# Decay logits as one 128-row matmul and gate columns made later in a one-core encoder layer

## The chip, the core and the metric

The kernel runs on one core of a Trainium2 chip. The metric is the device time of one execution in microseconds (us), lower is better. The core has a tensor engine (PE, with its weight loads listed as PEld), a vector engine (DVE), a scalar engine (ACT), GpSimd (POOL) and a sync engine (SP) that here only issues DMAs. Each engine works through its own queue in order; semaphores tie the queues together.

## The reference, cut to what matters

Two sequences of 256 tokens (stacked here to 512 columns) pass through one layer of width 1024: a feed-forward block, a mixer, a second feed-forward block and a norm. The mixer adds a gated linear attention (GLA, four heads) and an mLSTM (four heads), each scanned forwards and backwards. The change is in the gates of the two:

```python
# GLA: decay logits per direction from a 16-wide projection lr, then log-sigmoid
lr_f, lr_b = jnp.split(lr, [GLA_LOWRANK], axis=-1)
la_f = jax.nn.log_sigmoid((lr_f @ w2_f + b2_f).astype(f32)) / GLA_TAU
la_b = jax.nn.log_sigmoid((lr_b @ w2_b + b2_b).astype(f32)) / GLA_TAU
# mLSTM: two input gates and two forget gates per head
ig_f, lf_f = gates[:, :, 0], jax.nn.log_sigmoid(gates[:, :, 1])
ig_b, lf_b = gates[:, :, 2], jax.nn.log_sigmoid(gates[:, :, 3])
```

## The kernel before, in words

All tokens lie along the free dimension: a tile is 128 features by 512 tokens. To keep float32 accuracy with the faster `fp32r` matmul, each operand is split into a rounded high part (ACT copies it to `fp32r`) and the rest as low part (DVE subtracts), and a product is the sum of three matmuls: high by high, high by low, low by high (`mm3`, lines 202 to 204, with weights split in `split_w`, lines 93 and 94).

The order of work within each engine is not written by hand. A planner takes the program in text order and gives each engine, as it becomes free in the planner's own model of time, the earliest instruction in the text that is ready; the resulting queues are fixed in the program. An instruction is also held until a buffer of its kind is free. Tiles named `z`, `cc_ps`, `gA`, `gB`, `ops_g` and `mS` share four score buffers in PSUM (`scp`), given out in the order of the text.

The stretch around the change, in text order:
- The first feed-forward block ends; for each of its eight output tiles ACT makes the split input of the mixer and the squares, and POOL adds up the squares (`add_sq`, line 199).
- The mixer's pools open (lines 409 to 419): `w2s` (the second factor of the decay projection, one tile per direction), masks, and two zeroed tiles `zz`. Their DMAs are issued from POOL. Then the row norm (`rms_stat`: matmuls `st_m` line 160 and `sp_m` line 173) and the gemm `small`, whose result `ss` has in rows 0 to 31 the 16-wide projections of both directions, in rows 32 to 63 the same again, and from row 64 the mLSTM gates.
- Lines 430 to 438: rows 0 to 31 of `lr` are the high part of the projection, rows 32 to 63 the low part. `w2h` (64 rows) holds the high part of the factor twice, `w2l` (32 rows) its low part.
- `gla_half(0)` (heads 0 and 1): for each head the gemms of query and key, then `gla_prep`, where for each direction two matmuls (lines 519 and 520, 64 and 32 rows) make the decay logits `z`; ACT and DVE turn them into running sums and scaled queries and keys. Then the values gemm (`values`, `gemm_t`: lines 460 to 462, with `whi_vg` and `wlo_vg`), then `gla_weights` (`gA`, `gB`) and `gla_values` (`ops_g`).
- Gate rows of the mLSTM (lines 606 to 660), a long chain of small DVE operations on 8 rows, ending in `gR` (ACT, line 659) and `gN`. Lines 661 to 666: four matmuls turn `gR` into columns `cc_ps`, which DVE copies to `cc`. Line 669: `gN` goes to DRAM, from where the mLSTM part reads it broadcast.
- `gla_half(1)` (heads 2 and 3), line 671, then the mLSTM part, whose weights (`mlstm_weights`, line 717) read `cc` and the broadcast `gN`.

Of the kernel before, what the change touches and what calls it, by code (L numbers as in the profile page):

```python
# [9 lines left out]
F32 = mybir.dt.float32  # L10
F32R = mybir.dt.float32r
I32 = mybir.dt.int32
AF = mybir.ActivationFunctionType
ALU = mybir.AluOpType
# [4 lines left out]
T = 512  # L19
# [17 lines left out]
def encoder_kernel(ctx: ExitStack, tc: tile.TileContext, xT, par, w2, gnorm, mask,  # L37
                   w_f1, w_o1, w_small, w_mix, w_tm, w_out, w_f2, w_o2, out):
    nc = tc.nc
# [6 lines left out]
    dp = ctx.enter_context(tc.tile_pool(name="dp", bufs=1, space=bass.MemoryType.DRAM))  # L46
# [4 lines left out]
    @contextmanager  # L51
    def pools(**sizes):
        with ExitStack() as es:
            for n, b in sizes.items():
                stage[n] = es.enter_context(tc.tile_pool(name=f"{n}_{len(opened)}", bufs=b, reuse_waits="tile"))
                opened.append(n)
            yield
            for n in sizes:
                del stage[n]
# [3 lines left out]
    def slab(name, dt=F32, shape=(P, T)):  # L63
        return sp.tile(list(shape), dt, tag="slab", name=name)

    def mslab(name, dt=F32, shape=(P, T)):
        return stage["ms"].tile(list(shape), dt, tag="mslab", name=name)
# [4 lines left out]
    def mtmp(name, shape=(P, T)):  # L72
        return stage["mt"].tile(list(shape), F32, tag="mtmp", name=name)
# [7 lines left out]
    def scp(name, shape=(P, T)):  # L81
        return pc.tile(list(shape), F32, tag="sc", name=name)
# [55 lines left out]
    def col(c):  # L138
        return pt[:, c:c + 1]
# [75 lines left out]
    def gemm(src, xs, name, wide=False):  # L215

        ps = acc(f"ps_{name}", wide)
        for k, (hi, lo) in enumerate(chunks(src, len(xs), name)):
            mm3(ps, hi, lo, xs[k][0], xs[k][1], k == 0, k == len(xs) - 1)
        return ps  # L220
# [187 lines left out]

    mixer_stage = ExitStack()
    mixer_stage.enter_context(pools(wp=3, ms=16, mt=6))  # L410
    w2s = [mslab(f"w2s{d}", F32, (64, T)) for d in range(2)]
    masks = mslab("masks", I32, (P, 4, P))
    cm, am = masks[:, 0:2, :], masks.bitcast(F32)[:, 2:4, :]
    zz = [mslab(f"zz{i}", F32, (P, 4, P)) for i in range(2)]
    for z in zz:
        nc.gpsimd.memset(z, 0.0)
    for d in range(2):
        nc.gpsimd.dma_start(w2s[d], w2[:, d * T:(d + 1) * T])
    nc.gpsimd.dma_start(masks, mask)
    rm, rc_m = rms_stat(sqm, "m")  # L420
    rcol = cp.tile([P, 4], F32, name="rcol")
# [5 lines left out]
    ss = slab("ss")  # L427
    nc.vector.tensor_tensor(out=ss, in0=ps, in1=rm, op=ALU.mult)

    lr, lrh = slab("lr", F32R, (64, T)), slab("lrh", F32R, (64, T))  # L430
    nc.scalar.copy(lr[0:32, :], ss[0:32, :])
    nc.scalar.copy(lrh[32:64, :], ss[32:64, :])
    nc.vector.tensor_tensor(out=lr[32:64, :], in0=ss[32:64, :], in1=lrh.bitcast(F32)[32:64, :], op=ALU.subtract)
    w2h = [slab(f"w2h{d}", F32R, (64, T)) for d in range(2)]
    w2l = [slab(f"w2l{d}", F32R, (32, T)) for d in range(2)]
    for d in range(2):
        nc.scalar.copy(w2h[d], w2s[d])
        nc.vector.tensor_tensor(out=w2l[d], in0=w2s[d][0:32, :], in1=w2h[d].bitcast(F32)[0:32, :], op=ALU.subtract)

    def neg_softplus(dst_m, dst_l, src, bias):  # L440

        with tc.issue_after(log_exp):
            nc.scalar.activation(dst_l, src, AF.Abs, bias=bias)
            nc.scalar.activation(dst_l, dst_l, AF.Exp, scale=-1.0)
            nc.scalar.activation(dst_l, dst_l, AF.Ln, bias=1.0)
        nc.vector.tensor_scalar(out=dst_m, in0=src, scalar1=bias, scalar2=0.0, op0=ALU.add, op1=ALU.min)
# [67 lines left out]
    def gla_prep(h, qh, kh):  # L514
        E = []
        for d in range(2):
            zp = scp(f"z{d}{h}")
            f = slice(h * P, (h + 1) * P)
            nc.tensor.matmul(zp, lhsT=w2h[d][:, f], rhs=lr[0:64, :], start=True, stop=False)
            nc.tensor.matmul(zp, lhsT=w2l[d][:, f], rhs=lr[0:32, :], start=False, stop=True)  # L520
            m_, l_ = mtmp(f"zm{d}{h}"), mtmp(f"zl{d}{h}")
            neg_softplus(m_, l_, zp, col(C_B2 + 4 * d + h))
            b = mtmp(f"zb{d}{h}")
            for c in range(4):
                s = slice(c * P, (c + 1) * P)
                o_, i0, i1 = b[:, s], m_[:, s], l_[:, s]
                if d:
                    o_, i0, i1 = o_[:, ::-1], i0[:, ::-1], i1[:, ::-1]
                nc.vector.tensor_tensor_scan(out=o_, data0=i0, data1=i1, initial=0.0,
                                             op0=ALU.add, op1=ALU.subtract)  # L530
            b4 = b.rearrange("p (c t) -> p c t", t=P)

            qc, kc = (1, 0) if d == 0 else (0, 1)
            edge = (P - 1) if d == 0 else 0
            ex = mslab(f"ex{d}{h}", F32, (P, 2, 2, P))
            eq = mslab(f"eq{d}{h}", F32, (P, 4, P))
            ek = mslab(f"ek{d}{h}", F32, (P, 4, P))
            q4 = qh.rearrange("p (c t) -> p c t", t=P)
            k4 = kh.rearrange("p (c t) -> p c t", t=P)
            nc.scalar.activation(ex[:, 0], b4[:, qc::2, :], AF.Exp, scale=TAU_INV)  # L540
            nc.vector.tensor_tensor(out=ex[:, 1], in0=b4[:, kc::2, :],
                                    in1=b4[:, kc::2, edge:edge + 1].broadcast_to([P, 2, P]), op=ALU.subtract)
            nc.scalar.activation(ex[:, 1], ex[:, 1], AF.Exp, scale=-TAU_INV)
            nc.vector.tensor_tensor(out=ek, in0=b4, in1=b4[:, :, 63 + d:64 + d].broadcast_to([P, 4, P]),
                                    op=ALU.subtract)
            nc.scalar.activation(eq, ek, AF.Exp, scale=TAU_INV)
            nc.scalar.activation(ek, ek, AF.Exp, scale=-TAU_INV)
            nc.vector.tensor_tensor(out=eq, in0=eq, in1=q4, op=ALU.mult)
            nc.vector.tensor_tensor(out=ek, in0=ek, in1=k4, op=ALU.mult)
            nc.vector.tensor_tensor(out=ex[:, 0], in0=ex[:, 0], in1=q4[:, qc::2, :], op=ALU.mult)  # L550
            nc.vector.tensor_tensor(out=ex[:, 1], in0=ex[:, 1], in1=k4[:, kc::2, :], op=ALU.mult)
            E.append((eq, ek, ex))
        return E
# [24 lines left out]
    def gla_values(h, v):  # L578
        for q in range(2):
            hi, lo = pp_g[h][q]  # L580
            ops = scp(f"ops_g{q}{h}", (P, 2, SEQ))
            for c in range(2):
                pv(ops[:, c, :], [((hi[:, 2 * s + c, :], lo[:, 2 * s + c, :]), [p[:, h % 2, :] for p in v[2 * q + s]])
                                  for s in range(2)])
            for c in range(2):
                nc.scalar.copy(o_slot(0, h, 2 * q + c), ops[:, c, :])
                head_sq(0, h, 2 * q + c, ops[:, c, :])

    def gla_half(n):
        E = {}  # L590
        for h in (2 * n, 2 * n + 1):
            qh, kh = slab(f"gq{h}"), slab(f"gk{h}")
            nc.vector.scalar_tensor_tensor(out=qh, in0=gemm(w_mix[h], xsm, f"gq{h}"), scalar=DK_SCALE, in1=rm,
                                           op0=ALU.mult, op1=ALU.mult)
            nc.vector.tensor_tensor(out=kh, in0=gemm(w_mix[4 + h], xsm, f"gk{h}"), in1=rm, op=ALU.mult)
            E[h] = gla_prep(h, qh, kh)
        v = values(n, f"vg{n}", False)
        pp_g.extend(gla_weights(h, E[h]) for h in (2 * n, 2 * n + 1))
        for h in (2 * n, 2 * n + 1):
            gla_values(h, v)  # L600
# [5 lines left out]
    def grow(name, w=T):  # L606
        return slab(name, shape=(8, w)) if w == T else cp.tile([8, w], F32, name=name)

    gI, gM, gL, gF, gF2, gN = (grow(n) for n in ("gI", "gM", "gL", "gF", "gF2", "gN"))
# [28 lines left out]
    for q in range(2):  # L638
        for (c, tot) in ((2 * q, gT), (2 * q + 1, gT2)):
# [6 lines left out]
                                op=ALU.add)  # L646
# [5 lines left out]
                                in1=gT2[:, 2 * q + 1:2 * q + 2], op=ALU.add)  # L652
# [5 lines left out]
    nc.vector.tensor_scalar(out=gN2, in0=gN2, scalar1=-88.0, scalar2=None, op0=ALU.max)  # L658
    nc.scalar.activation(gE, gN2, AF.Exp, scale=-1.0)
    nc.vector.tensor_scalar(out=gN, in0=gN, scalar1=-1.0, scalar2=None, op0=ALU.mult)  # L660
    cc_ps = scp("cc_ps", (P, 4, 24))
    for t in range(4):
        nc.tensor.matmul(cc_ps[:, t, :], lhsT=gR[:, t * P:(t + 1) * P], rhs=pt[:, C_ROW:C_ROW + 24],
                         start=True, stop=True)
    cc = cp.tile([P, 3, 4, 8], F32, name="cc")
    nc.vector.tensor_copy(cc.rearrange("p i t r -> p t i r"), cc_ps.rearrange("p t (i r) -> p t i r", i=3))

    d_nm = dp.tile([8, T], F32, name="d_nm")
    nc.gpsimd.dma_start(d_nm, gN)

    gla_half(1)
    head_r = [head_rms(0), None]


# [148 lines left out]
    for kp in range(4):  # L823
        t = (w_raw, w_sum)[kp % 2](f"second{kp}").rearrange("p a b -> p (a b)")
        t = t.rearrange("p (i m f) -> p i m f", i=2, m=NF)
# [131 lines left out]
```

## Time and profile before

| | us |
|---|---|
| Median of 3 runs | 1236.21 (1231.79 to 1238.27) |
| The profiled execution | 1234.58 |
| Span of its trace | 1232.8 |
| PE busy in the span | 1190.1 |
| DVE busy | 765.1 |
| ACT busy | 609.3 |
| POOL busy | 100.5 |
| Mean granted clock of PE | 0.983 of 2.4 GHz |

Times in the profile count from the start of the span. A row of the timeline gives the start, the duration, the engine, the line of the kernel, the operation, the tile written and the tiles read, and behind that the time its engine sat idle before it and what ended that. Matmuls are pipelined, so the distance from one start to the next says more than the duration shown. The granted clock is 1.00 for 2.4 GHz and 0.50 for 1.2 GHz.

### The profile page before, as it was taken

The numbers are of one execution on the slowest core, as the hardware profiler recorded it, in microseconds if no ns is written. First come the engines' busy times: TensorE is split into PE (matmuls) and PEld (weight loads), VectorE is DVE, ScalarE is ACT, GpSimd is POOL, SyncE is SP. The second block draws the span as 40 slices with busy tenths as digits, with TensorE's granted clock in tenths as the row PEclk, the third lists the DMA queues.
The fourth block names the chain that finished last, engine by engine and source line by source line (L and its number), as shares of the span: only waits on it lengthen the run. The fifth ranks groups of instructions, "written<-read, shape, count | busy, mean of one in ns | idle before, by whom it ended". The sixth has DMA issues, their size and how long they took to land.

```text
span 1232.8 us, 17190 instructions
## 1 busy us (share of the span) xinstructions
PE 1190.1 (97%) x6803; PEld 1035.0 (84%) x6803; DVE 765.1 (62%) x1159; ACT 609.3 (49%) x995; POOL 100.5 (8%) x114
## 2 busy tenths in 40 slices
PE   8899999999999999999999999999989999999996
PEld 6788899889987786888888888887879899989985
DVE  7976467557646788647565354464886457656643
ACT  5664256336536545566663232353565146426541
POOL 4000000000021002111000000012000000000011
PEclk9889999999999998999999999998999999999998
DMA  7355256436513212232323333224355246535512
GB/s 234 78 135 147 95 129 163 126 114 154 139 67 120 81 48 64 91 121 65 98 73 98 101 96 111 86 69 116 88 139 154 89 116 165 145 99 147 153 45 69
DMA packets 56737, 136.52 MB, mean 111 GB/s; under 512 B 5160, under 2 KB 19496, under 8 KB 56656
## 3 DMA queue, kind: packets, MB, share of 16 engines
q1 hardware_dynamic: 48480, 110.38, 28.1%
q0 software_dynamic: 6368, 22.68, 10.7%
q10 hardware_dynamic: 1808, 2.36, 0.6%
q8 instruction: 53, 0.87, 0.3%
q14 instruction: 28, 0.23, 0.1%
HBM read 133.29 MB, written 2.11 MB: 110 GB/s over the span
## 4 chain that ended last, share of the span: by engine, by line
PE 85%; DVE 6%; issue 3%; ACT 3%; DMA 2%; POOL 0%; POOLq 0%; DVEq 0%; SPq 0%; ACTq 0%
PE psy_f L302 17%; PE psq_f L302 8%; PE psz_f L302 4%; PE ps_f1o L202 3%; PE ps_f1o L203 3%; PE ps_f1o L204 3%; PE ps_f2o L203 3%; PE ps_f2o L202 3%; PE ps_f2o L204 3%; PE pt_ga L461 2%; PE pt_ga L460 2%; PE pt_ga L462 2%; PE pt_gb L461 2%; PE pt_gb L460 2%; PE pt_gb L462 2%
## 5 line engine op out<-in xcount | busy, mean ns | idle before, releaser
L302 PE MATMUL psy_f<-xch_f,wah_f1s 128*128 128x256 f32 x228 | 65.5, 287 | 3.8 <-DVE f1t L321 1.4
L302 PE MATMUL psy_f<-xch_f,wal_f2s 128*128 128x256 f32 x228 | 64.9, 285 | 4.2 <-DMA wal_f2s<-in_w_f 4.2
L302 PE MATMUL psy_f<-xch_f,wah_f2s 128*128 128x256 f32 x228 | 64.8, 284 | 0.1
L302 PE MATMUL psy_f<-xch_f,wal_f1s 128*128 128x256 f32 x228 | 64.6, 284 | 0.0
L302 PE MATMUL psy_f<-xcl_f,wah_f2s 128*128 128x256 f32 x228 | 64.5, 283 | 0.0
L302 PE MATMUL psy_f<-xcl_f,wah_f1s 128*128 128x256 f32 x228 | 64.5, 283 | 0.0
L460 PE MATMUL pt_ga<-whi_ga,xh_m 128*128 128x512 f32 x128 | 50.7, 396 | 0.0
L461 PE MATMUL pt_ga<-wlo_ga,xh_m 128*128 128x512 f32 x128 | 50.7, 396 | 0.0
L461 PE MATMUL pt_gb<-wlo_gb,xh_m 128*128 128x512 f32 x128 | 50.7, 396 | 0.0
L460 PE MATMUL pt_gb<-whi_gb,xh_m 128*128 128x512 f32 x128 | 50.5, 395 | 0.0
L462 PE MATMUL pt_ga<-whi_ga,xl_m 128*128 128x512 f32 x128 | 50.4, 394 | 0.0
L462 PE MATMUL pt_gb<-whi_gb,xl_m 128*128 128x512 f32 x128 | 50.2, 394 | 0.0
L94 DVE TENSOR_TENSOR wlo_ga<-raw_ga,whi_ga 128x1024 fp32r<-128x1024 f32 x16 | 19.6, 1225 | 46.2 <-ACT whi_ga L93 46.2
L302 PEld LDWEIGHTS psy_f<-xch_f,wah_f1s 128*128 128x128 f32 x228 | 43.8, 192 | 5.0 <-DVE f1t L321 1.7
L302 PEld LDWEIGHTS psy_f<-xch_f,wal_f2s 128*128 128x128 f32 x228 | 43.5, 191 | 4.6 <-DMA wal_f2s<-in_w_f 4.6
L385 DVE SCALAR_TENSOR_TENSOR x<-ps_f2o,x 128x512 f32<-128x512 f32 x23 | 15.9, 690 | 49.6 <-PE ps_f2o L204 49.6
L302 PEld LDWEIGHTS psy_f<-xcl_f,wah_f1s 128*128 128x128 f32 x228 | 44.0, 193 | 0.1
L385 DVE SCALAR_TENSOR_TENSOR x<-ps_f1o,x 128x512 f32<-128x512 f32 x24 | 16.6, 690 | 44.3 <-PE ps_f1o L204 44.3
L302 PEld LDWEIGHTS psy_f<-xch_f,wah_f2s 128*128 128x128 f32 x228 | 43.4, 190 | 0.6 <-ACT f2m L351 0.5
L302 PEld LDWEIGHTS psy_f<-xch_f,wal_f1s 128*128 128x128 f32 x228 | 43.7, 192 | 0.0
L302 PEld LDWEIGHTS psy_f<-xcl_f,wah_f2s 128*128 128x128 f32 x228 | 43.4, 190 | 0.1
L94 DVE TENSOR_TENSOR wlo_gb<-raw_gb,whi_gb 128x1024 fp32r<-128x1024 f32 x16 | 19.6, 1224 | 36.1 <-ACT whi_gb L93 36.0
(1083 smaller groups left out, 4052.4 us busy)
## 6 DMA issues: line engine op xcount, KB each, us to landing
raw_f1s<-in_w_f SPq DMA_DIRECT2D x19, 512.0 KB, 3.6
wal_f1s<-in_w_f POOLq DMA_DIRECT2D x19, 512.0 KB, 5.7
raw_f2s<-in_w_f SPq DMA_DIRECT2D x19, 512.0 KB, 3.6
wal_f2s<-in_w_f POOLq DMA_DIRECT2D x19, 512.0 KB, 5.5
raw_ga<-in_w_tm SPq DMA_DIRECT2D x16, 512.0 KB, 3.6
raw_gb<-in_w_tm SPq DMA_DIRECT2D x16, 512.0 KB, 3.5
sum_f1s<-in_w_f SPq DMA_DIRECT2D x19, 256.0 KB, 3.3
raw_f1s<-in_w_f SPq DMA_DIRECT2D x19, 256.0 KB, 4.0
```

What stands on the lines that cost most here:

```text
L94: nc.vector.tensor_tensor(out=lo[:, :width], in0=raw[:, :width], in1=hi.bitcast(F32)[:, :width], op=ALU.subtract)
L202: nc.tensor.matmul(ps, lhsT=wh, rhs=xh, start=start, stop=False)
L203: nc.tensor.matmul(ps, lhsT=wh, rhs=xl, start=False, stop=False)
L204: nc.tensor.matmul(ps, lhsT=wl, rhs=xh, start=False, stop=stop)
L302: nc.tensor.matmul(ps, lhsT=l[:, f], rhs=m, start=start and k == n == 0, stop=stop and k == 3 and n == 2, skip_group_check=True)
L385: nc.vector.scalar_tensor_tensor(out=x[i], in0=ps, scalar=0.5, in1=x[i], op0=ALU.mult, op1=ALU.add)
L460: nc.tensor.matmul(pss[t], lhsT=xh, rhs=hi[:, ws], start=k == 0, stop=False)
L461: nc.tensor.matmul(pss[t], lhsT=xh, rhs=lo[:, ws], start=False, stop=False)
L462: nc.tensor.matmul(pss[t], lhsT=xl, rhs=hi[:, ws], start=False, stop=k == KD - 1)
```

## The change

The three products of the decay logits, which were two matmuls (64 rows: high and low part of `lr` by the high part of the factor; 32 rows: high part by the low part), are put on top of each other in one matmul of 128 rows. Rows 64 to 95 of the moving operand repeat the high part of `lr` and meet the low part of the factor; rows 96 to 127 are zero on both sides. For this `w2s` becomes 128 rows high, is filled by two DMAs per direction and a POOL memset of its last 32 rows, and `lr` gets two more ACT copies. The four matmuls of `cc_ps` and the copy to `cc` move behind `gla_half(1)` in the text; the DMA of `gN` stays ahead of it.

```diff
-    w2s = [mslab(f"w2s{d}", F32, (64, T)) for d in range(2)]
+    w2s = [mslab(f"w2s{d}") for d in range(2)]
...
     for d in range(2):
-        nc.gpsimd.dma_start(w2s[d], w2[:, d * T:(d + 1) * T])
+        nc.gpsimd.memset(w2s[d][96:128, :], 0.0)
+        nc.gpsimd.dma_start(w2s[d][0:64, :], w2[:, d * T:(d + 1) * T])
+        nc.gpsimd.dma_start(w2s[d][64:96, :], w2[0:32, d * T:(d + 1) * T])
     nc.gpsimd.dma_start(masks, mask)
...
-    lr, lrh = slab("lr", F32R, (64, T)), slab("lrh", F32R, (64, T))
+    lr, lrh = slab("lr", F32R), slab("lrh", F32R, (64, T))
     nc.scalar.copy(lr[0:32, :], ss[0:32, :])
     nc.scalar.copy(lrh[32:64, :], ss[32:64, :])
+    nc.scalar.copy(lr[64:96, :], ss[0:32, :])
+    nc.scalar.copy(lr[96:128, :], zz[0].rearrange("p c t -> p (c t)")[96:128, :])
     nc.vector.tensor_tensor(out=lr[32:64, :], in0=ss[32:64, :], in1=lrh.bitcast(F32)[32:64, :], op=ALU.subtract)
-    w2h = [slab(f"w2h{d}", F32R, (64, T)) for d in range(2)]
-    w2l = [slab(f"w2l{d}", F32R, (32, T)) for d in range(2)]
+    w2x = [slab(f"w2x{d}", F32R) for d in range(2)]
     for d in range(2):
-        nc.scalar.copy(w2h[d], w2s[d])
-        nc.vector.tensor_tensor(out=w2l[d], in0=w2s[d][0:32, :], in1=w2h[d].bitcast(F32)[0:32, :], op=ALU.subtract)
+        nc.scalar.copy(w2x[d], w2s[d])
+        nc.vector.tensor_tensor(out=w2x[d][64:96, :], in0=w2s[d][64:96, :], in1=w2x[d].bitcast(F32)[64:96, :],
+                                op=ALU.subtract)
...
-            nc.tensor.matmul(zp, lhsT=w2h[d][:, f], rhs=lr[0:64, :], start=True, stop=False)
-            nc.tensor.matmul(zp, lhsT=w2l[d][:, f], rhs=lr[0:32, :], start=False, stop=True)
+            nc.tensor.matmul(zp, lhsT=w2x[d][:, f], rhs=lr, start=True, stop=True)
...
     nc.vector.tensor_scalar(out=gN, in0=gN, scalar1=-1.0, scalar2=None, op0=ALU.mult)
+
+    d_nm = dp.tile([8, T], F32, name="d_nm")
+    nc.gpsimd.dma_start(d_nm, gN)
+
+    gla_half(1)
+
     cc_ps = scp("cc_ps", (P, 4, 24))
     for t in range(4):
         nc.tensor.matmul(cc_ps[:, t, :], lhsT=gR[:, t * P:(t + 1) * P], rhs=pt[:, C_ROW:C_ROW + 24],
                          start=True, stop=True)
     cc = cp.tile([P, 3, 4, 8], F32, name="cc")
     nc.vector.tensor_copy(cc.rearrange("p i t r -> p t i r"), cc_ps.rearrange("p t (i r) -> p t i r", i=3))
-
-    d_nm = dp.tile([8, T], F32, name="d_nm")
-    nc.gpsimd.dma_start(d_nm, gN)
-
-    gla_half(1)
     head_r = [head_rms(0), None]
```

## Rows read from the trace of the kernel before

**Rows 1.** The page: busy us, share of the span and instructions of each engine.
```profile
PE 1190.1 (97%) x6803; PEld 1035.0 (84%) x6803; DVE 765.1 (62%) x1159; ACT 609.3 (49%) x995; POOL 100.5 (8%) x114
```
**Rows 2.** Timeline around the first head's z, on PE and PEld.
```profile
394.30 0.39 PE L203 MATMUL ps_gk<-xl_m,whi_gk 128*128 128x512 f32 x1
394.53 0.40 PE L204 MATMUL ps_gk<-xh_m,wlo_gk 128*128 128x512 f32 x1
394.85 0.50 PE L519 MATMUL z<-lr,w2h 64*128 64x512 f32 x1
395.28 0.18 PEld L520 LDWEIGHTS z<-lr,w2l 32*128 32x128 f32 x1 [0.25 <-issue]
395.29 0.49 PE L520 MATMUL z<-lr,w2l 32*128 32x512 f32 x1
395.71 0.50 PE L519 MATMUL z<-lr,w2h 64*128 64x512 f32 x1
...
396.89 0.40 PE L203 MATMUL ps_gq<-xl_m,whi_gq 128*128 128x512 f32 x1
```
**Rows 3.** Timeline of PE, starts around z of the second and fourth heads.
```profile
407.55 0.40 PE L204 MATMUL ps_gk<-xh_m,wlo_gk 128*128 128x512 f32 x1
...
409.91 0.40 PE L461 MATMUL pt_vg<-wlo_vg,xh_m 128*128 128x512 f32 x1
...
472.70 0.39 PE L204 MATMUL ps_gk<-xh_m,wlo_gk 128*128 128x512 f32 x1
...
475.05 0.40 PE L461 MATMUL pt_vg<-wlo_vg,xh_m 128*128 128x512 f32 x1
```
**Rows 4.** Timeline of PE from the wait for gR to full pace.
```profile
461.12 0.40 PE L202 MATMUL ps_gk<-xh_m,whi_gk 128*128 128x512 f32 x1
...
463.22 1.62 PE L663 MATMUL cc_ps<-pt,gR 128*128 128x24 f32 x8 [1.71 <-ACT gR L659]
...
464.77 0.79 PE L519 MATMUL z<-lr,w2h 64*128 64x512 f32 x1
...
465.49 0.79 PE L520 MATMUL z<-lr,w2l 32*128 32x512 f32 x1
...
470.38 0.40 PE L203 MATMUL ps_gk<-xl_m,whi_gk 128*128 128x512 f32 x1
```
**Rows 5.** Windows: busy us per engine (instructions), granted clock, DMA share, GB/s.
```profile
447.38:491.61 44.23, 41.37 (x164) 31.26 (x164) 39.34 (x87) 21.38 (x35) 4.76 (x5) 0.92 0.19 58
...
463.57:470.40 6.83, 6.83 (x18) 4.45 (x18) 3.99 (x9) 3.79 (x7) 0.04 (x1) 0.50 0.28 79
```
**Rows 6.** Timeline of PE: eight small fp32 passes at full clock.
```profile
432.01 1.05 PE L561 MATMUL gA<-eq,ek 128*128 128x128 f32 x8
```
**Rows 7.** Timeline of POOL ahead of the mixer, and PE's st_m.
```profile
375.79 0.53 POOL L416 MEMSET zz<- 128x512 f32 x1 [0.80 <-PE ps_f1o L203]
...
376.26 1.11 POOL L418 DMA_DIRECT2D w2s<-in_w  x2
...
377.34 0.59 POOL L419 DMA_DIRECT2D masks<-in_mask  x1
...
378.12 1.51 POOL L199 TENSOR_TENSOR sqm<-sqm,sq_m 128x512 f32<-128x512 f32 x1 [0.18 <-ACT sq_m L198]
...
379.68 1.05 PE L160 MATMUL st_m<-ones,sqm 128*128 128x1 f32 x8 [0.25 <-POOL sqm L199]
```
**Rows 8.** Timeline of the second values gemm: third cast, first start, third subtract.
```profile
472.89 1.05 ACT L93 CAST whi_vg<-raw_vg 128x1024 fp32r<-128x1024 f32 x1 [1.87 <-PE ps_gk L203]
...
474.71 0.50 PE L460 MATMUL pt_vg<-whi_vg,xh_m 128*128 128x512 f32 x1
...
487.67 1.19 DVE L94 TENSOR_TENSOR wlo_vg<-raw_vg,whi_vg 128x1024 fp32r<-128x1024 f32 x1
...
488.92 0.50 PE L461 MATMUL pt_vg<-wlo_vg,xh_m 128*128 128x512 f32 x1 [1.15 <-DVE wlo_vg L94]
```
**Rows 9.** Timeline of ACT ahead of the first z.
```profile
387.99 0.62 ACT L432 CAST lrh<-ss 32x512 fp32r<-32x512 f32 x1
388.63 1.14 ACT L437 CAST w2h<-w2s 64x512 fp32r<-64x512 f32 x2
```

## The prediction

> **What bounds the kernel now.** The first view is the page's line of busy times: the tensor engine (PE) is busy for 1190.1 of 1232.8 us, every other engine for 62% or less [rows 1]. So a change counts if it shortens PE's own queue or one of the few stretches in which PE waits. The change touches one stage, the mixer's opening (about 376 to 500 us), so I read that stage in PE's order of time and compare start to start, because the durations shown for matmuls overlap. In the steady gemms a 128-row matmul starts 0.23 us after the one before (394.30 to 394.53 [rows 2]).
>
> Two things in the stage are slower than that. First, the decay logits z: around them the starts are 0.42 to 0.44 us apart, and their weight load does not run ahead as the others do; it starts with its matmul after 0.25 us in which nothing the profile shows is waited for [rows 2]. Second, the columns cc: at 461.12 PE starts one matmul of the fourth key gemm, then stands 1.71 us for gR, the last of the gate rows, runs eight passes of cc in 1.62 us, and everything behind them is slow: z is 0.72 us apart, and only at 470.38 is the next gemm step fast again [rows 4]. The windows view says why: in 463.57 to 470.40 the granted clock is 0.50, so 1.2 GHz, although PE is never idle in it [rows 5]. It fell after the idle time and the tiny matmuls, and rose after some microseconds of gap-free matmuls.
>
> **The change part by part: the packed matmul.** Each of the eight z (four heads, two directions) loses one of two matmuls, and the one left has 128 rows like its neighbours. Three of the four places lie at full clock.
> - First head: 394.53 to 396.89, 2.36 us for six starts [rows 2]; four starts of 0.23 remain, 0.92. Saved 1.44.
> - Second head: 407.55 to 409.91, also 2.36 [rows 3]. Saved 1.44.
> - Fourth head: 472.70 to 475.05, 2.35 [rows 3]. Saved 1.43.
> Together 4.31 us, all on PE. Bounds: if the packed matmul keeps 0.42 spacing (a rival below), each place gives only 2 x 0.42 = 0.84.
>
> Of the width of these matmuls the rows say that 64 and 32 rows with the same 512 columns cost 0.42 to 0.44 and 128 rows 0.23 [rows 2]. The Trainium skill, TensorE: Matmul & The Clock Gate, section LDWEIGHTS (loading the stationary operand), says that a load's time goes by columns and not by rows, so that 32 rows cost what 128 do; by that alone the change would drop eight starts of 0.23, 1.8 us, over all four places. The trace disagrees with that reading, and the skill's TensorEngine Tiling (Array Packing), section Key Properties, has the other half: changing the tiling mode drains the engine. By the second rule the 0.19 extra goes from the remaining z too; the sum above goes by the rows.
>
> **The moved cc.** From 461.12 to 470.38 is 9.26 us [rows 4]. Without cc and with two z there, the same stretch is nine starts (two z and seven gemm steps, to the one at 470.38): 9 x 0.23 = 2.07. Saved 7.19: 1.71 of idle, 1.62 of cc, the half clock and two z. The cc passes come back behind the second half. No row shows them at full clock; the nearest are eight small fp32 passes of gA, 1.05 [rows 6], and the eight of st_m, 1.05 [rows 7]; below, nothing can make it negative, since the passes must run; above, 1.62 as they are now [rows 4]. I take 1.05. Its inputs are by then long done (gR was awaited at 461, and the second half ends after 500), the planner has the next gemm for PE meanwhile, and the DVE copy of cc is first read by the exponentials of the mLSTM weights, after the values gemm. The DMA of gN to DRAM now stands ahead of the half in the text; POOL has nothing between, so it costs nothing.
>
> PE's sum: 4.31 + 7.19 - 1.05 = 10.45 us. The third head's z is no longer behind cc in the queue for score buffers, so it can move from 464.77 to right behind its key gemm, where the first head's stands.
>
> **What is late next: DVE.** Take 447.38 (first gate scan) to 491.61 (the end of the last subtract, `wlo_vg`, that the values gemm needs): 44.23 us, in which DVE is busy 39.34 [rows 5]. PE's queue in it would shrink by 7.19 and 1.43, and by the 1.15 it waits for `wlo_vg` now [rows 8], to 34.46. If all that DVE work must come first, the stretch cannot go under 39.34 and saves 4.89 instead of 9.77; then the total is 1.44 + 1.44 + 4.89 - 1.05 = 6.72. If none of it binds, the total is 10.45, or 11.6 with the 1.15 gone. The gemm itself needs only its four subtracts; the rest (scans and products of two heads) is for gA behind it. For the cap speaks that `whi_vg` of the third chunk was cast from 472.89 but its subtract came only at 487.67, behind scans [rows 8]. Against it speaks that the third head's preparation can now start some ten us earlier and fill DVE's idle time. I take the middle of 6.72 and 10.45: 8.6.
>
> **What it adds.** ACT gets two copies more (ss into rows 64 to 95, zeros into 96 to 127): 0.62 each by the 32-row copy [rows 9], so w2's casts end near 391.0 instead of 389.77 and the two DVE subtracts (1.28 together) by 391.8 or so. The first z starts at 394.85 [rows 2]: 3 us of cover. The casts and subtracts themselves keep their length, having as many columns. If that cover were gone, 1.2 us would go to the path.
>
> POOL gets two memsets (0.53 by that of zz, which has more rows; below, not under 0) and two more DMA issues (0.555 each, 1.11 for two [rows 7]), up to 2.2 us. Queued behind them on POOL are the masks' issue and then the last sum of squares, L199, for which PE's st_m stands in line [rows 7]. POOL was free at 377.93 and L199 started at 378.12, so 0.2 us of cover. If all goes ahead of L199, PE stalls 2.0 us more at st_m; if the planner serves L199 (earlier in the text) as soon as it is ready, at most one issue is ahead of it, 0 to 0.55. I take 0.3. The masks and the DMA'd rows have slack: w2's cast is at 388.63 [rows 9].
>
> Those POOL issues took 0.555 us each with DVE's subtracts running beside them [rows 7]. The Trainium skill, SBUF — State Buffer, sections SBUF: two separate sides and A bandwidth-pool intuition that's wrong, speaks against adding them: POOL can be locked out by some DVE copies while it writes descriptors, 3.1 us instead of 0.62. By that two issues would hold L199 for about 6 us, and the second rival would cost 4 us more; the trace does not show it.
>
> **The sum.** 8.6 - 0.3 = 8.3 us. The profiled execution took 1234.58, so 1226.3. The median of the runs is 1236.21, 1.63 above it; behind the stage PE is the bound too [rows 1], so I carry the saving through and predict 1227.9 us.
>
> **Rivals.**
> - **PE alone decides** (20%): DVE keeps ahead. 10.45 to 11.6 saved: 1224.6 to 1225.8. For it: PE is the bound everywhere else [rows 1].
> - **A new stall takes the old one's place** (22%): POOL's four added steps hold L199 and PE waits at st_m, or cc waits for a score buffer. Price: 1.7 more than taken, and if the clock falls as it did after 1.71 us of idle, half of 6.83 at 0.50 [rows 5], 3.4. Saved 8.3 - 5.1 = 3.2: 1233.0.
> - **The packing does not do what it says** (4%): z keeps 0.42 spacing. Each place loses 0.6: 8.3 - 2.4 = 5.9 saved, 1230.3. Against it: its form is that of its neighbours.
> - **Slower: the values gemm starves** (7%). The third head's preparation, set free, runs together with the gate rows and the fourth head's, and the planner puts all of it ahead of `wlo_vg`. DVE's 39.34 less three subtracts of 1.2 is 35.7; begun at 447.38 less 2.9, it ends at 480.2; 96 matmuls of 0.23 follow, 22.1, to 502.3, then cc 1.05 and a clock fall 3.4: 506.8, where the gemm now ends near 499.3. 7.5 us slower, 1243.7. It decides from the point where the first `wlo_vg` is later than 474.71, the gemm's first start now [rows 8]; before that some gain is left. Against it: gA of the third head could fill PE.
> - The forecast has 47%, about 1225 to 1231.
>
> **The numbers.** About 0.5%, 6.2 us, is what a measurement of this kernel can tell from no change; so faster means under 1230.0. Most of the forecast (0.43), PE alone (0.20) and a little of the rest give 0.66; the new stall, the packing and the forecast's tail give 0.27 for the same; slower 0.07. The range runs from 1221.5 (11.6 saved and about 3 of run-to-run spread) to 1235.5, which takes in the new stall and leaves out the starved gemm.
>
> **What would show it.** Right: eight z matmuls of 128x512 at 0.23 spacing; no PE idle and clock 1.00 near 450 to 470; cc passes after 490 in about 1.05; z of the third head right behind its key gemm. Cap: waits of PE for `wlo_vg` of 1 to 4 us between 460 and 485. New stall: PE idle over 1 us before st_m, or a clock of 0.50 near 380. Wrong: a shift elsewhere, in either FFN, as large as this stage's.

## The result and the profile after

Median 1228.04 us (1226.0 to 1231.72, six runs) against 1236.2 (1231.79 to 1238.42, six runs) for the kernel before: ratio 0.9936, 95% interval 0.992 to 0.9952. The forecast was 1227.9. The profiled execution took 1228.9 us, its span is 1227.1.

The page's line of busy times (after): PE is still the bound, busy for 6.7 us less than in [rows 1].
```profile
PE 1183.4 (96%) x6795; PEld 1031.8 (84%) x6795; DVE 763.8 (62%) x1159; ACT 609.6 (50%) x997; POOL 105.6 (9%) x118
```
Timeline of PE (after) around the first head's logits, then the third head's:
```profile
396.38 0.39 PE L204 MATMUL ps_gk<-xh_m,wlo_gk 128*128 128x512 f32 x1
396.61 0.63 PE L523 MATMUL z<-lr,w2x 128*128 128x512 f32 x2
397.08 0.40 PE L202 MATMUL ps_gq<-xh_m,whi_gq 128*128 128x512 f32 x1
397.31 0.39 PE L203 MATMUL ps_gq<-xl_m,whi_gq 128*128 128x512 f32 x1
...
452.93 0.39 PE L204 MATMUL ps_gk<-xh_m,wlo_gk 128*128 128x512 f32 x1
453.16 0.63 PE L523 MATMUL z<-lr,w2x 128*128 128x512 f32 x2
453.63 0.40 PE L202 MATMUL ps_gq<-xh_m,whi_gq 128*128 128x512 f32 x1
```
From 396.38 to 397.31 four starts take 0.93 us, where [rows 2] has six in 2.36. The third head's z, at 464.77 in [rows 4], now stand right behind their key gemm, at 453.16, and there is no wait for gR. But PE meets another wait. Timeline of PE (after) around the first subtract of the values gemm, and the windows view (PE, PEld, DVE, ACT, POOL busy, granted clock, DMA share, GB/s) of 20 us there, of the half-clock stretch, and of the stretch from the first gate scan to the last `wlo_vg`:
```profile
465.20 0.86 PE L464 MATMUL pt_vg<-whi_vg,xh_m 128*128 128x512 f32 x3
468.71 0.80 PE L465 MATMUL pt_vg<-wlo_vg,xh_m 128*128 128x512 f32 x1 [2.64 <-DVE wlo_vg L94]
...
471.75 0.40 PE L464 MATMUL pt_vg<-whi_vg,xh_m 128*128 128x512 f32 x1
```
```profile
464.00:484.00 20.00, 17.36 (x81) 14.11 (x81) 20.00 (x42) 12.53 (x23) 5.75 (x2) 0.91 0.24 70
468.30:471.70 3.40, 2.99 (x7) 2.41 (x8) 3.40 (x8) 3.40 (x8) 0.00 (x0) 0.52 0.41 142
446.40:484.90 38.50, 35.86 (x161) 29.10 (x160) 38.22 (x88) 21.30 (x35) 7.17 (x3) 0.96 0.19 55
```
PE stands 2.64 us for `wlo_vg`, then runs at about half clock for 3.4 us (half of that, 1.7, lost by estimate). DVE is busy all through. Why the subtract is late, its queue shows. Timeline of ACT and of DVE (after): the cast that `wlo_vg` needs, and steps of DVE's queue between it and the subtract.
```profile
453.13 1.05 ACT L93 CAST whi_vg<-raw_vg 128x1024 fp32r<-128x1024 f32 x1 [4.51 <-PE ps_gk L203]
```
```profile
455.86 0.67 DVE L596 SCALAR_TENSOR_TENSOR gq<-ps_gq,r_m 128x512 f32<-128x512 f32 x1
...
461.47 0.41 DVE L663 TENSOR_SCALAR gN<-gN 8x512 f32<-8x512 f32 x1
...
466.50 1.04 DVE L532 TENSOR_TENSOR_SCAN zb<-zm,zl 128x128 f32<-128x128 f32 x3
467.47 1.19 DVE L94 TENSOR_TENSOR wlo_vg<-raw_vg,whi_vg 128x1024 fp32r<-128x1024 f32 x1
```
The cast was done by 454.2; the subtract starts at 467.47, behind 13 us of gate rows (gN) and of the third head's preparation (gq, zb).

The columns cc at their new place, and POOL ahead of the mixer with PE's matmuls that wait for it (after):
```profile
504.47 0.97 PE L672 MATMUL cc_ps<-pt,gR 128*128 128x24 f32 x8
505.28 0.47 PE L204 MATMUL ps_mq<-xh_m,wlo_mq 128*128 128x512 f32 x1
```
```profile
378.00 0.52 POOL L418 MEMSET w2s<- 32x512 f32 x1
378.48 0.56 POOL L419 DMA_DIRECT2D w2s<-in_w  x1
379.02 0.55 POOL L420 DMA_DIRECT2D w2s<-in_w  x1
379.75 1.50 POOL L199 TENSOR_TENSOR sqm<-sqm,sq_m 128x512 f32<-128x512 f32 x1 [0.18 <-ACT sq_m L198]
381.31 0.52 POOL L418 MEMSET w2s<- 32x512 f32 x1
...
381.31 1.05 PE L160 MATMUL st_m<-ones,sqm 128*128 128x1 f32 x8 [0.48 <-POOL sqm L199]
```
cc takes 0.81 us to the next start and waits for nothing. The last sum of squares (L199) started 0.18 us after POOL came free, with only one direction's memset and DMAs ahead of it, and what it waited for was ACT's `sq_m`. Timeline of PE, the last gemm step ahead of `st_m` before, and the same after:
```profile
379.03 0.40 PE L204 MATMUL ps_small<-xh_m,wlo_small 128*128 128x512 f32 x1
```
```profile
380.43 0.40 PE L203 MATMUL ps_small<-xl_m,whi_small 128*128 128x512 f32 x1
```
Counted from PE's first `ps_small` (375.80 before, 377.43 after), L199 starts 2.32 us and `st_m` 3.88 us later in both profiles. So POOL's new steps held neither back. PE waits 0.48 and not 0.25 because the planner put 14 matmuls of `ps_small` ahead of `st_m` where there were 15.

**A measure for the experiments.** The time at which the mixer starts differs from execution to execution (375.8 in the profile before, 377.4 after, and 377.7, 377.9 and 378.5 in three kernels below whose program is as before up to there). So profiles are compared by the *stage*, from PE's first `ps_small` to its first `mS` of the mLSTM part, and by the *way to tr*, from the same start to PE's first transpose `tr` ahead of the mixer's out projection, where what was only put off has come back. Before: 178.6 and 428.1 us. After: 171.4 and 421.1.

Each stage is read from one execution, and part of it runs at half clock: 6.8 us in before and cc alone, 3.4 in after, packing alone, the second full matmul and cc not moved, none in the other kernels of the table. About half of that time is lost, so two stages can differ by 1.7 or 3.4 us through the clock alone.

| kernel | median us | before, same chip | ratio (95%) | stage | way to tr |
|---|---|---|---|---|---|
| before | | | | 178.6 | 428.1 |
| after | 1228.04 | 1236.2 | 0.9936 (0.992 to 0.9952) | 171.4 | 421.1 |
| packing alone | 1227.2 | 1236.04 | 0.993 (0.9914 to 0.9946) | 171.6 | 421.3 |
| cc moved alone | 1233.01 | 1236.04 | 0.9974 (0.9961 to 0.9988) | 176.8 | 426.6 |
| a second full matmul per z | 1231.93 | 1236.04 | 0.9956 (0.9942 to 0.9971) | 174.0 | 424.3 |
| subtracts first | 1228.64 | 1236.04 | 0.9934 (0.992 to 0.9948) | 169.5 | 419.5 |
| subtracts and reads first | 1225.76 | 1235.4 | 0.9923 (0.9908 to 0.9937) | 168.3 | 417.9 |
| the same, cc not moved | 1230.38 | 1236.27 | 0.9952 (0.9933 to 0.9971) | 171.6 | 421.4 |
| gate rows moved too | 1226.5 | 1235.4 | 0.9931 (0.9915 to 0.9946) | 167.4 | 418.5 |
| the same, w2 from host | 1224.67 | 1235.4 | 0.9918 (0.9903 to 0.9934) | 167.1 | 418.9 |
| rows and cc moved, no packing | 1232.45 | 1235.4 | 0.9972 (0.996 to 0.9985) | 172.9 | 425.5 |

### The profile page after: what moved, and what is told of

The parts are those of the page before. It is cut to its first block, busy times and chain, and to the rows that moved or that the text cites. A ratio compares the mean times of both kernels' runs of the same rounds, so it can differ in the third digit from the quotient of the medians.

```text
span 1227.1 us, 17179 instructions
## 1 busy us (share of the span) xinstructions
PE 1183.4 (96%) x6795; PEld 1031.8 (84%) x6795; DVE 763.8 (62%) x1159; ACT 609.6 (50%) x997; POOL 105.6 (9%) x118
## 3 DMA queue, kind: packets, MB, share of 16 engines
q10 hardware_dynamic: 1808, 2.36, 0.6%
## 4 chain that ended last, share of the span: by engine, by line
PE 86%; DVE 8%; ACT 2%; DMA 2%; issue 1%; POOL 0%; POOLq 0%; DVEq 0%; SPq 0%; ACTq 0%
PE psy_f L302 17%; PE psq_f L302 8%; PE psz_f L302 4%; PE ps_f1o L202 3%; PE ps_f1o L203 3%; PE ps_f1o L204 3%; PE ps_f2o L203 3%; PE ps_f2o L202 3%; PE ps_f2o L204 3%; PE pt_ga L465 2%; PE pt_ga L464 2%; PE pt_ga L466 2%; PE pt_gb L465 2%; PE pt_gb L464 2%; PE pt_gb L466 2%
```

## The experiments

### Each part alone

Packing alone: the kernel after, with cc put back ahead of the second half.
```diff
+    cc_ps = scp("cc_ps", (P, 4, 24))
...
     d_nm = dp.tile([8, T], F32, name="d_nm")
     nc.gpsimd.dma_start(d_nm, gN)
     gla_half(1)
-    cc_ps = scp("cc_ps", (P, 4, 24))
...
```


> The changed kernel with the cc matmuls put back ahead of the second linear attention half. If the two parts add up as in the prediction: the packed z saves 4.3 us at its three full-clock places and two starts of 0.72 at the slow one, less 0.3 for POOL, so 5.4 us, about 1230.8; PE still waits 1 to 2 us for gR and the clock is at 0.50 behind it. Rival, that all of the gain came from moving cc: 1235 to 1237. Rival, that the packing is all of it: 1228.

Moving cc alone: the kernel before, with the same lines moved the other way and z left as two matmuls of 64 and 32 rows.
```diff
-    cc_ps = scp("cc_ps", (P, 4, 24))
...
     gla_half(1)
+    cc_ps = scp("cc_ps", (P, 4, 24))
...
```


> The kernel before with only the cc matmuls moved behind the second half; z stays at 64 and 32 rows. By PE's queue alone: the slow stretch of 9.26 us becomes about 3.5 (six starts in 2.36 with four z, five more of 0.23), less 1.05 for cc elsewhere, so 4.7 us saved, 1231.5. If the subtracts for the second values gemm come late as in the changed kernel (a wait of 2.6 us and a fall of the clock), only 1 to 2 us are left: 1234 to 1235. Rival, that moving cc is all of the gain: 1228.

Measured: packing alone 1227.2 us, ratio 0.993, as much as the whole change; moving cc alone 1233.01, ratio 0.9974. Timeline of PE (packing alone) at cc, and the waits of PE there (us in total, times, longest):
```profile
461.14 0.40 PE L202 MATMUL ps_gk<-xh_m,whi_gk 128*128 128x512 f32 x1
463.27 1.07 PE L667 MATMUL cc_ps<-pt,gR 128*128 128x24 f32 x8 [1.73 <-ACT gR L662]
464.18 1.12 PE L523 MATMUL z<-lr,w2x 128*128 128x512 f32 x2
465.10 0.63 PE L203 MATMUL ps_gk<-xl_m,whi_gk 128*128 128x512 f32 x1
...
467.66 0.41 PE L203 MATMUL ps_gk<-xl_m,whi_gk 128*128 128x512 f32 x1
```
```profile
PE pt_vg L465 <- DVE wlo_vg L94: 1.1, 1, 1.1
```
The wait for gR stands as in [rows 4]. From 461.14 to 467.66 the stretch takes 6.52 us where it took 9.26: z costs less, and the half clock holds for 3.4 us and not for 6.8. That is 2.74; with 4.3 at the other three heads 7.0, which is the stage's gain (178.6 to 171.6). Up to 1.7 of it is the shorter half clock, and one execution of each doesn't show that the packing shortened it.

So from there the change after should have gained 6.52 - 2.07 - 0.81 = 3.6 us more by moving cc. It gained 0.2 (171.6 to 171.4). Its wait for `wlo_vg` is 1.5 longer than here (2.64 against 1.1) and the half clock behind it loses 1.7: 3.2 of the 3.6. With cc alone moved, PE likewise waits for DVE. Waits of PE and a window (cc alone):
```profile
PE pt_vg L460 <- DVE gk L595: 1.0, 1, 1.0
PE pt_vg L461 <- DVE wlo_vg L94: 0.3, 1, 0.3
```
```profile
472.80:479.60 6.80, 6.43 (x14) 4.75 (x15) 6.80 (x12) 4.73 (x10) 0.58 (x1) 0.50 0.50 147
```
There 6.8 us run at half clock, as long as in [rows 5]: the wait for gR is gone, the half clock that stood behind it is not. The median lies between the two that were expected.

### Is it the number of matmuls or the number of rows?

After, with a second matmul of 128 rows (zero weights) added to each z:
```diff
-            nc.tensor.matmul(zp, lhsT=w2x[d][:, f], rhs=lr, start=True, stop=True)
+            nc.tensor.matmul(zp, lhsT=w2x[d][:, f], rhs=lr, start=True, stop=False)
+            nc.tensor.matmul(zp, lhsT=wz, rhs=lr, start=False, stop=True)
```


> The changed kernel with a second matmul at each z, 128 rows of zeros by the same moving operand, so that each z has two matmuls again, both of 128 rows (the sum is the same). If 64 and 32 rows were slow because the row count changes from one matmul to the next: spacing 0.23 everywhere and 8 x 0.23 = 1.9 us more on PE than the changed kernel, 1228 to 1230. Rival, that a second matmul into the same z buffer is what costs 0.42: each place takes 2.36 again, the packing's gain is gone, 1232 to 1234.

Timeline of PE (second full matmul):
```profile
397.78 0.39 PE L526 MATMUL z<-lr,w2x 128*128 128x512 f32 x1
398.01 0.39 PE L527 MATMUL z<-lr,wz 128*128 128x512 f32 x1
398.24 0.39 PE L526 MATMUL z<-lr,w2x 128*128 128x512 f32 x1
```
Two matmuls into one buffer, in the same order as before, and 0.23 apart, here and at all other z (16 starts in 3.69 us). So the 0.42 to 0.44 of [rows 2] belonged to the 64- and 32-row form, and not to accumulating twice. The loads themselves are no longer with few rows (0.18 us at 32 rows in [rows 2]); they only don't run ahead. Whether few rows cost this by themselves, or only the change between 64 and 32, no run here tells apart. The stage grew by 2.6 us against after: four heads of two extra starts are 1.8, the rest lies in the waits for DVE, which here sum to 3.3 us (gk 1.7, gq 1.0, `wlo_vg` 0.6). The median, 1231.93, would by itself suit the rival (1232 to 1234) better; the spacing is what decides.

### DVE: its amount of work or its order?

The forecast's cap took the DVE work up to the last subtract as a fixed amount. After, with only the subtracts of the second values gemm put ahead of all else on DVE.
```diff
-            hi, lo = split_w(raw, f"{name}_{kp}")
+            if name == "vg1":
+                with tc.high_priority():
+                    hi, lo = split_w(raw, f"{name}_{kp}")
+            else:
+                hi, lo = split_w(raw, f"{name}_{kp}")
```


> The changed kernel, with the casts and subtracts of the second values gemm given priority over the preparation of the heads. If the order of DVE's queue is what costs (wait of 2.64 us for wlo_vg and 1.7 us of half clock behind it): both gone, 4.3 us less than the changed kernel, about 1223.7, and no wait of PE over 0.5 us between 440 and 500. Rival, that DVE's work as a whole is the bound there: a wait of about the same size moves to gA or the next gemm, 1227 to 1229. Rival, that the heads' preparation is then late: over 1230.

The wait changed its name and kept its size, now for the read of the last query gemm, whose buffer the values gemm needs. Waits of PE, and a window (subtracts first):
```profile
PE pt_vg L468 <- DVE gq L600: 2.6, 1, 2.6
```
```profile
464.00:484.00 20.00, 17.40 (x75) 13.75 (x74) 19.97 (x40) 12.97 (x22) 2.69 (x4) 1.00 0.31 93
```
By this alone DVE's amount of work seems to decide, and the median (1228.64) lies where that rival had it. In this execution the clock stayed at 1.00 after the wait, which accounts for most of the stage's 1.9 us. The next kernel gave the reads of those query and key gemms the same rank:
```diff
+            pq = gemm(w_mix[h], xsm, f"gq{h}")
+            with (tc.high_priority() if n else ExitStack()):
+                nc.vector.scalar_tensor_tensor(out=qh, in0=pq, scalar=DK_SCALE, in1=rm, op0=ALU.mult, op1=ALU.mult)
+            pk = gemm(w_mix[4 + h], xsm, f"gk{h}")
+            with (tc.high_priority() if n else ExitStack()):
+                nc.vector.tensor_tensor(out=kh, in0=pk, in1=rm, op=ALU.mult)
```


> After the change, with the second values gemm's subtracts and the reads of the query and key gemms of heads 2 and 3 both put ahead of all else on DVE. If the order on DVE is what holds PE, both waits (2.64 for wlo_vg, 2.60 for gq) go and the median is near 1224. If DVE's total work is, a wait of 2 to 3 us turns up at the next reader (gA or the head norms), the stage stays at 169 to 172 and the median at 1227 to 1229.

Windows of the same 20 us, and of the stretch from the first gate scan to the last `wlo_vg`; then the wait that is left (subtracts and reads first):
```profile
464.00:484.00 20.00, 20.00 (x87) 16.17 (x86) 20.00 (x41) 13.14 (x22) 2.42 (x3) 1.00 0.33 93
...
447.10:477.20 30.10, 30.10 (x131) 24.41 (x130) 29.80 (x69) 16.40 (x25) 0.53 (x1) 1.00 0.25 71
```
```profile
PE gA L568 <- DVE zz L575: 1.4, 1, 1.4
```
DVE is as full as before, and PE no longer waits in the stretch. The last subtract ends 30.1 us after the first gate scan, not 38.5; the scans and products that stood ahead of it were not needed by the values gemm and came later. So the order was what held PE at the values gemm, and not the amount. But gA then waits 1.4 for DVE, so about half of the 2.64 turns up at the next reader. The stage is 168.3, 10.3 less than before and 3.1 less than after, and the way to tr 417.9. Of the 3.1, 1.7 is the half clock, which didn't come here; with the subtracts alone put first it didn't come either, and the wait of 2.6 was still there. The median, 1225.76, lies between the two expected. By the whole time the kernel is not told apart from the change: 0.9923 (0.9908 to 0.9937) against 0.9936 (0.992 to 0.9952).

The same ranks with cc left at its old place (both edits above on the kernel with packing alone) say what cc's move is worth once DVE's order doesn't take it back.

> Packing alone (cc still ahead of the second half), with the same reads put first on DVE as in reads_first. Theory (moving cc adds nothing to the packing only because DVE's order takes its gain back): the wait for gR stays or grows (1.7 us with packing alone), as the rows are now behind those reads; the stage is 170 to 172 against 168.3 in reads_first, the median 1227 to 1229 against 1225.8. Rival (cc's place is worth nothing once the logits are packed): stage 168 to 169, median 1225 to 1226.

PE's waits in the stage (subtracts and reads first, cc not moved):
```profile
PE cc_ps L674 <- ACT gR L669: 1.9, 1, 1.9
PE gA L568 <- DVE zz L575: 1.0, 1, 1.0
```
The wait for gR stays. Stage 171.6 against 168.3: 3.3 us, near the 3.6 worked out above, and 1.7 of it is the half clock behind that wait. The same move was worth 0.2 us with DVE in the planner's order. The median, 1230.38, is above the 1227 to 1229 expected, and 3.2 above packing alone, whose stage is as long; the ratios' intervals (0.9933 to 0.9971 and 0.9914 to 0.9946) overlap, and the first of them just overlaps that of the subtracts and reads first.

### The gate rows moved too

After, with the whole DVE chain of the gate rows, from the scans of gF on, behind the second half:
```diff
+    gla_half(1)
...
     nc.gpsimd.dma_start(d_nm, gN)
-    gla_half(1)
     cc_ps = scp("cc_ps", (P, 4, 24))
```


> After the change, with the DVE chain of the gate rows (from the scans of gF to gN and gR, about 11 us of DVE work) moved behind the second linear attention half as well, ahead of cc. Theory (DVE's total work between the first gate scan and the values gemm's last subtract is what holds PE): the wait for wlo_vg (2.64 in the changed kernel) and the clock fall behind it (3.41 us at half clock, 1.7 us lost) go, the stage from the first ps_small start to the first mS start shrinks from 171.4 to about 167, the median is near 1223.7. Rival (the rows' work only changes place): the 11 us come back as DVE or ACT waits ahead of cc, mS or the head norms of the mLSTM, the stage stays at 170 to 173, the median at 1227 to 1230.

Stage 167.4, as the theory had it: no DVE wait and no half clock in it. But the median is 1226.5 and not 1223.7, and the way to tr is only 2.6 us shorter than after, where the stage is 4.0 shorter. Waits of PE, and POOL's timeline (gate rows moved too):
```profile
PE pm L492 <- POOL vh_vm L482: 1.6, 2, 0.8
PE cc_ps L673 <- ACT gR L664: 0.5, 1, 0.5
```
```profile
512.70 0.53 POOL L668 DMA_DIRECT2D d_nm<-gN  x1 [14.92 <-DVE gN L665]
...
555.50 1.33 POOL L701 TENSOR_TENSOR nmm<-nmb,masks 128x512 f32<-128x512 f32 x1 [3.13 <-DMA nmb<-d_nm]
556.77 1.26 POOL L482 CAST vh_vm<-unit 128x4 fp32r<-128x4 f32 x1
```
The DMA that takes gN to DRAM is issued at 512.70 now (462.17 after); the sums on POOL that read it back wait about 3 us each for their DMA (3 to 4 after, where three of them are done by 498), and a small cast that the mLSTM's product of values and weights (pm) needs stands behind one of them.

The same with the factor laid out in 128 rows by the host:
```diff
-        nc.gpsimd.memset(w2s[d][96:128, :], 0.0)
-        nc.gpsimd.dma_start(w2s[d][0:64, :], w2[:, d * T:(d + 1) * T])
-        nc.gpsimd.dma_start(w2s[d][64:96, :], w2[0:32, d * T:(d + 1) * T])
+        nc.gpsimd.dma_start(w2s[d], w2[:, d * T:(d + 1) * T])
```

> The same, and the factor of the decay logits laid out in 128 rows by the host, zeros included, so that POOL has no memset and one DMA per direction ahead of the last sum of squares. Theory: PE's wait for that sum ahead of st_m goes back from 0.48 to 0.25, 0.2 us off the sum of the kernel with the rows moved, so not to be told apart from it (1223.5 against 1223.7). Rival: POOL's steps ahead of the mixer cost more than that wait shows, 1 us or more.

1224.67 us, ratio 0.9918: `st_m` waits 0.3 again instead of 0.5, and stage and way (167.1, 418.9) are as without the host's layout. The medians' 1.8 us between the two are more than that wait shows; their intervals overlap widely, and I take them as the same.

To that, the small casts of the values taken from POOL:
```diff
-                nc.gpsimd.tensor_copy(hi[:, :, SEQ:], unit[:, 0:2, :])
-                nc.gpsimd.tensor_copy(lo[:, :, SEQ:], unit[:, 2:4, :])
+                nc.scalar.copy(hi[:, :, SEQ:], unit[:, 0:2, :])
+                nc.scalar.copy(lo[:, :, SEQ:], unit[:, 2:4, :])
```


> rows_later_host with the small casts of the ones and zeros columns of the mLSTM values on ACT and not on POOL. Theory (what rows_later gained at the stage's end, 4.0 us, and lost to 2.6 us by the first out projection, it lost to POOL, whose casts stand behind sums that wait for DMAs): the waits for vh_vm go, the way from ps_small to the first tr is 416.5 to 417.5 instead of 418.5 to 418.9, median about 1223. Rival: ACT's or DVE's part of the same values is as late, the waits change name, 418.5 and 1224.7.

Here 1226.61 us, ratio 0.9921 (0.9905 to 0.9937), stage 167.2, way to tr 418.7. The casts no longer hold pm, but PE now waits there for DVE and ACT steps of the same weights (0.8, 0.8 and 0.5 us). The rival held: what is made later is late for its next reader too, whoever makes the casts.

Last, the move of the rows and cc without packing: `gla_half(1)` set ahead of the rows in the kernel before, as in the first diff of this part.

> The kernel before, with the gate rows' chain and cc both behind the second half, and z still two matmuls of 64 and 32 rows. If DVE is what took back the gain of moving cc alone (stage 176.8 against 178.6), PE has neither the wait for gR nor one for wlo_vg or gk here, and the saving is 9.26 us less nine starts at their old spacing (two z at 0.72 become four at 0.43, the rest 0.23: 3.3) less cc 0.8: some 5 us, stage near 173, median near 1231. If DVE isn't, the stage stays at 176 to 177 and the median at 1233 to 1234.

Stage 172.9, 5.7 less than before, as expected (3.4 of it is the half clock, which didn't come); way to tr only 2.6 less, median 1232.45 and not 1231. Between `mS` and `tr` 3.1 us came back, and PE's waits at pm rose from 0.8 to 3.3.

### The best order

The kernel with subtracts and reads first, with the host's layout and the casts on ACT (the two diffs above).

> reads_first with the factor in 128 rows from the host and the small casts on ACT. st_m's wait back from 0.48 to 0.25; pm's issue gap of 0.8 stays or goes; way to the first tr 417.0 to 417.8 (417.9 in reads_first), median 1224.5 to 1225.5. If the casts on ACT delay the casts that PE waits for, over 418.5 and 1226.5.

1225.87 us, ratio 0.9914 (0.9896 to 0.9932), stage 168.0, way to tr 417.6, the shortest of all and as expected. Its interval and that of the change as made (0.992 to 0.9952) still overlap, so by the whole time it is not shown to be faster; by the stage it saves 3.4 us more, 1.7 of them the half clock.

### Why z stood behind cc

The kernel before, with cc_ps in the gemms' buffers instead of the score buffers:
```diff
-    cc_ps = scp("cc_ps", (P, 4, 24))
+    cc_ps = pa.tile([P, 4, 24], F32, tag="acc", name="cc_ps")
```


> The kernel before, with cc_ps in the buffers of the gemms in place of the four score buffers; nothing moved, nothing packed. Theory (the third head's z stood behind cc because score buffers are given out in the order of the text): z of the third head now comes right behind its key gemm, near 453, at 0.42 to 0.44 spacing, ahead of cc; the wait for gR stays at 1.5 us or more and the clock falls after it. Rival (z was late for its own inputs): z stays behind cc, near 465.

Timeline of PE (cc in another kind of buffer), and a window of the idle time:
```profile
445.81 0.49 PE L519 MATMUL z<-lr,w2h 64*128 64x512 f32 x1
...
448.78 0.49 PE L520 MATMUL z<-lr,w2l 32*128 32x512 f32 x1
466.13 1.90 PE L663 MATMUL cc_ps<-pt,gR 128*128 128x24 f32 x8 [16.86 <-ACT gR L659]
```
```profile
449.20:466.20 17.00, 0.14 (x2) 0.07 (x1) 16.01 (x48) 8.53 (x17) 0.22 (x1) 0.52 0.00 0
```
All eight z matmuls of the second half ran in a row, ahead even of its query and key gemms: z was held by the order of the score buffers and not by its inputs. They start 0.42 us apart with no 128-row matmul between them. What I had not seen: cc now holds a place in the gemms' line of buffers, and all gemms of the second half stood behind its wait, 16.9 us. The one execution took 1251.07 us, the stage 192.9. A wait of the same operation costs 1.7 or 16.9 us by which line it stands in.

## Why the prediction was right, point by point

The time came out at 1228.04 where 1227.9 was forecast, and that closeness is luck. The forecast is the median before, 1236.21, less 8.3 us. Between the medians 8.2 us were saved, but the ratio's interval leaves 5.9 to 9.9, and the stage, where the change acts, gained 7.2 and not 8.3. Between the two profiled executions it is 5.7 (1234.58 to 1228.9), as the mixer began 1.6 us later in the second.

The stage's 7.2, by the steps of the sum: 4.3 of packing at three heads, plus 7.19 for the slow stretch, less 0.81 of cc, less 1.49 of longer waiting for `wlo_vg` (2.64 against 1.15 in [rows 8]), less 1.7 of half clock, less 0.23 at `st_m`, makes 7.26. The 1.7 is half of 3.4; seven starts there (468.71 to 471.75) took 3.04 us, 1.4 more than at 0.23, and with that the sum is 7.6, so some 0.3 us lie elsewhere in the stage.

- **The packed matmul: right.** 1.43 saved at the first head, 1.44 forecast; the second full matmul shows that the form was the cause.
- **The slow stretch: right where it was, but over a third of it isn't cc's.** With cc in place, packing alone takes 2.74 of its 7.19, up to 1.7 of it through a shorter half clock.
- **cc at its new place: mis-sized.** 0.81 us, where 1.05 was taken from the passes of gA.
- **POOL: the size near, the reason wrong.** 0.23 more at `st_m` against 0.3. But no added step held L199, which started as long after the mixer's first matmul as before; `st_m` was put one gemm step earlier in PE's queue (with w2 from the host it has its old place and waits 0.26 again). That the size fits is luck.
- **ACT's added copies: no cost seen.** The first z follows its key gemm at 0.23.
- **The cap: its size right, its reason wrong.** The stretch took 38.5 us, with DVE busy in 38.22, against a cap of 39.34: as long as if the cap bound in full, and the middle of 8.6 was the step that failed. But it was no amount of work that must come first. With the reads and subtracts put first the stretch took 30.1 us, and 1.4 us of waiting for DVE moved on to gA. What bound is the queue as the planner made it: gate rows and the third head's preparation, earlier in the text, ahead of the subtract that PE waits for. Rows of before showed that too (the third chunk cast from 472.89 and subtracted from 487.67 [rows 8]).
- **The half clock moved.** It was priced as gone (clock 1.00 near 450 to 470); behind the new wait it came back for 3.4 us. The forecast had it in a rival alone.
- **The rivals.** The new stall, at `st_m` or cc, did not come. The wait that came, 2.64 us for `wlo_vg` at 468.71, is the one that the forecast named as the sign of its cap; with the clock's fall behind it, which the cap did not price, it cost 3.2 us (1.49 and 1.7). The starved gemm would have needed a first `wlo_vg` after 474.71; it came at 467.47. PE alone was not reached by the change; the kernel with the reads first came to it (10.3 in the stage against 10.45).

What stays open: why the clock fell behind some waits and not behind others of the same size (below), and whether the kernels with the best stages are faster than after as a whole. Their medians gained up to 2 us less against after than their way to tr did. One source of such differences is in the traces: behind tr the clock falls again, for a time that changes from execution to execution. Windows of 30 us there, after and then packing alone:
```profile
840.00:870.00 30.00, 27.22 (x106) 21.57 (x106) 17.16 (x32) 11.68 (x19) 2.58 (x2) 0.89 0.47 137
```
```profile
840.00:870.00 30.00, 27.22 (x120) 21.45 (x119) 18.96 (x35) 12.30 (x19) 3.38 (x3) 1.00 0.48 141
```
In the best order the clock of this window is 0.83. From tr to the end the three traces take 428.6, 425.6 and 430.0 us. How much of this is in the medians, one trace of each kernel doesn't show.

## What to carry to other kernels

Price the two halves of a change apart and then together: here packing took 7.0 us off the stage and moving cc 1.8 by themselves, and 7.2 as a pair, since what the second saved on PE was lost again waiting for DVE. When a wait of the bound engine is taken away, look in the queue of the engine that feeds it for the first operand that is ready early and served late, and rank that one: with no work removed on a full DVE, the stage went from 171.4 to 168.3 us (1.7 of it the half clock), and moving cc was worth 3.3 us there in place of 0.2. Count waits and half clock apart, and don't take one trace's half clock for the kernel's. A matmul that contracts few rows may be cheaper with zero rows up to 128, when its neighbours have 128 (here 0.23 in place of 0.42 to 0.44 us).

## What the runs showed of the hardware

- A matmul of 64 or 32 rows by 512 columns cost 0.42 to 0.44 us from start to start among 128-row ones (before), and 0.42 on average in a row of eight without such between (cc in another kind of buffer); one of 128 rows cost 0.23, also when two fill the same buffer one after the other.
- The granted clock fell to 0.50 behind PE waits of 1.71, 1.73, 1.93 and 16.86 us for gR followed by small passes, behind 2.64 for `wlo_vg`, behind 1.00 for gk (cc alone), and behind 1.02, 1.70 and 0.64 in a row (second full matmul); it stayed at 1.00 behind 2.60 for gq and 1.44 at gA. It stayed low for 3.4 us in four of these profiles and for 6.8 in two (before, and cc alone), so much the same wait costs about 1.7 or 3.4 us more by this alone.
- POOL's DMA issues ahead of the mixer took 0.51 to 0.56 us each in the kernel after, and 0.56 and 0.59 in [rows 7], with DVE at work beside them.
